# Two attention sink terms per pair of heads: from two ScalarE exponentials to one VectorE subtraction and one ScalarE exponential

## The chip, the cores and the metric

The kernel runs on one core of a Trainium2 chip. The metric is device time in microseconds (us) of one execution. Engines are named as in the profile: PE is TensorE's matmuls and PEld its weight loads, DVE is VectorE, ACT is ScalarE, POOL is GpSimd, SP is SyncE, whose queue issues the DMAs.

## The reference

Two layers, each one mixer sub-layer over 1024 latent tokens and 256 context tokens of width 1024, in float32: a modulated RMS norm, one input projection to 2560 columns, three parallel branches (attention with 8 heads of 64, a depthwise convolution, a Fourier branch), each times a SiLU gate, one output projection, a gated residual. Only the attention's softmax matters here. Each block of 128 queries sees at most 384 local keys and the 256 context keys, and one more logit per head that has no value row, the sink:

```
s_sink = broadcast(sink.reshape(1, 1, N_KV_HEADS, GQA_GROUP, 1, 1))
p = softmax(concatenate([s_loc, s_ctx, s_sink], axis=-1), axis=-1)
```

So the denominator of a row is the sum of the exponentials of its 640 (or fewer) scores plus `exp(sink - max)`, where the maximum goes over scores and sink. That last term, one number per query and head, is what the change computes in another way.

## The kernel before

Every large product is split into three single-pass products of rounded halves, so PE carries most of the work: the input projection (lines 198 to 200) in 128x512 matmuls over eight blocks of the width, the output projection by the same lines.

Attention is a list of steps, one for each block of 128 queries and pair of heads: 40 steps in the first layer, 32 in the second, 72 in all. A step makes scores (PE, lines 899 and 901) into one of two PSUM tiles of two banks each; takes the negated maximum (`maxima`, DVE); makes the exponentials (`exponentials`, ACT, line 925), whose sum comes with a read of the accumulator; makes the two sink terms (`sinks`, ACT, line 933); adds and inverts (`divide`, two DVE operations of 128x2) and multiplies the exponentials by the inverse on POOL (line 941). One step later PE transposes the result (line 955), ACT copies the rounded half (`ph`, line 960), DVE takes the rest (`pl`); one more step later PE multiplies by the values (line 969). A score tile is free for the next head when its exponential has been read.

The signs are turned: the score tiles hold negated scores, so the maximum is a minimum, `st[:, j]` holds minus the maximum of head `j`, and `nsink` holds minus the sink logits of all 16 heads of both layers in every partition. The small tile `st` (128x10) of a step holds minus the maxima in columns 0 and 1, the sink terms, later the denominators, in 2 and 3, the sums in 4 and 5, the inverses in 6 and 7.

Between two steps stands a piece of other work: half a projection, splits of weights, the output projection of a block whose attention is done. The function `step` writes the order of a program, but what runs is the order that a list scheduler makes of it: it places each instruction on its engine by readiness in its own model of the machine, with the program's order as priority. Each engine then runs its list strictly in order. A moved instruction can therefore move others far from it, on every engine.

All VectorE operations go through a helper and carry line 57 in the profile, so they are told apart by the names of what they write: `st<-` with no source is the read of a maximum, `st<-st` of 128x2 the addition or the reciprocal of `divide`.

Of the kernel before, what the change touches and what calls it, by code (L numbers as in the profile page):

```python
# [15 lines left out]
AF = mybir.ActivationFunctionType  # L16
ALU = mybir.AluOpType
# [13 lines left out]
NH = 8  # L31
# [108 lines left out]
def tile_backbone(ctx: ExitStack, tc: tile.TileContext, a, out):  # L140
    nc = tc.nc
    V, S, G, T = Behind(tc, nc.vector), nc.scalar, nc.gpsimd, nc.tensor
# [30 lines left out]
    def fill_v(us):  # L173
        p0 = tc.cur_priority
        tc.cur_priority = p0 + 300
        V.background = True
        while back and us > 0:
            t, f = back.popleft()
            f()
            us -= t  # L180
        V.background = False
        tc.cur_priority = p0
# [4 lines left out]
    def flush(q):  # L187
        for _ in range(len(q)):
            q.popleft()()
# [294 lines left out]
    class Pair:  # L484
# [6 lines left out]
        def step(self, blocks=range(NK)):  # L491
            for k in blocks:
                ks = slice(k * P, (k + 1) * P)
                for oo, w in zip(self.o, self.w):
                    mm3(oo, (w[0][:, ks], w[1][:, ks]), (hx[k][0].cols(*self.c), hx[k][1].cols(*self.c)),
                        k == 0, k == NK - 1)
# [338 lines left out]
    nsink = const.tile([P, DEPTH * NH], F32, name="nsink")  # L835
# [9 lines left out]
    class Attention:  # L845
# [82 lines left out]
        def sinks(self, i):  # L928
            z, pr = self.st[i], self.steps[i][1]
            st = z["st"]  # L930
            for j in range(2):
                h = self.l * NH + pr * 2 + j
                S.activation(st[:, 2 + j:3 + j], nsink[:, h:h + 1], AF.Exp, scale=-1.0, bias=st[:, j:j + 1])

        def divide(self, i):
            z = self.st[i]
# [58 lines left out]
        def step(self, fill=None):  # L995

            i, n = self.next, len(self.steps)
            if i == n + 2:
                return False
            self.next += 1  # L1000
            c, d = 0 <= i - 1 < n, 0 <= i - 2 < n
            flush(post)
            if i < n:
                b, pr = self.steps[i]
                self.scores(i)
                self.maxima(i, 0)
                if pr == 3:
                    self.q.pop(b)[0].put()
                if pr == 0:
                    self.load(i + 4)  # L1010
            if c:
                self.transpose(i - 1, 0)
            if i < n:
                self.maxima(i, 1)
                self.exponentials(i, 0)
            if c:
                self.transpose(i - 1, 1)
            if d:
                self.values(i - 2)
            if i < n:  # L1020
                self.exponentials(i, 1)
            if c:
                self.transpose(i - 1, 2)
            if d:
                self.output(i - 2)
            if i < n:
                self.sinks(i)
                self.divide(i)
                if pr == 2:
                    self.queries(i + 2)  # L1030
            flush(late)
            fill_v(2.5)
            if fill:
                fill()
            return True
# [637 lines left out]
```

## Time and profile before

| | before |
|---|---|
| median of 3 runs | 1176.14 us (1173.57 to 1181.28) |
| profiled execution | 1175.1 us, its span 1172.9 us |
| busy share of the span | PE 93%, PEld 79%, DVE 71%, ACT 46%, POOL 24% |
| chain that ended last | PE 73%, DVE 12%, DMA 7%, ACT 3% |
| mean granted clock of PE | 0.97 of full |

The page's first part gives the busy time of each engine, its fourth part the chain of work that ended last, followed back from the last instruction; the share of an engine in that chain is the time in which that engine held up the end. A wait is told as the engine and line that waited, then who released it. Attention runs from about 275 to 625 us in the first layer and from about 845 to 1140 us in the second.

### The profile page before, as it was taken

How to read it: one execution, taken by the hardware profiler on the slowest of the kernel's cores; microseconds unless marked ns; L12 is line 12 of the kernel's file. 1: busy time of each engine (PE TensorE's matmuls, PEld its weight loads, DVE VectorE, ACT ScalarE, POOL GpSimd, SP SyncE). 2: the span in 40 equal slices, each digit the busy share in tenths (PEclk: the TensorE clock that was granted, in tenths of full speed). 3: DMA queues.
4: the chain of work that ended last, by engine and by line, in shares of the span. 5: the costliest groups of instructions: out<-in, count | busy, mean ns of one | idle time of the engine just before them, and what ended most of it. 6: DMA issues, size and time to landing. Idle time of an engine off the chain costs nothing.

```text
span 1172.9 us, 17178 instructions
## 1 busy us (share of the span) xinstructions
PE 1095.1 (93%) x6165; PEld 923.6 (79%) x6165; DVE 828.8 (71%) x1702; ACT 541.5 (46%) x1195; POOL 285.7 (24%) x271
## 2 busy tenths in 40 slices
PE   5999999999999999899999999989889997999986
PEld 2688887778878988788888788868678886788865
DVE  4545998997776567767665269999566677577763
ACT  4442222215566555555557653222346555455551
POOL 1230000002222234344553220000131344234321
PEclk9999999999999999899999999999989997899989
DMA  9711238453322253336458423532423254433210
GB/s 333 230 61 55 90 111 235 149 193 81 86 87 75 79 161 98 97 113 205 161 191 269 141 60 107 169 114 72 108 63 86 91 149 127 116 108 91 91 54 36
DMA packets 150924, 144.90 MB, mean 124 GB/s; under 512 B 7302, under 2 KB 128566, under 8 KB 150840
## 3 DMA queue, kind: packets, MB, share of 16 engines
q1 hardware_dynamic: 150840, 143.82, 40.5%
q8 instruction: 48, 0.79, 0.3%
q14 instruction: 36, 0.29, 0.1%
HBM read 109.71 MB, written 34.09 MB: 123 GB/s over the span
## 4 chain that ended last, share of the span: by engine, by line
PE 73%; DVE 12%; DMA 7%; ACT 3%; issue 2%; SPq 2%; POOL 1%; DVEq 0%; ACTq 0%; POOLq 0%
PE mm L198 13%; PE mm L199 13%; PE mm L200 13%; PE mm L969 5%; PE pt L955 5%; PE pt L198 5%; PE pt L199 5%; PE pt L200 4%; PE score L899 2%; PE score L901 2%; DMA wr<-od 2%; DVE score L57 2%; DVE cy L57 2%; DMA wada<-w_ada 1%; DVE pl L57 1%
## 5 line engine op out<-in xcount | busy, mean ns | idle before, releaser
L198 PE MATMUL mm<-hxh,wh 128*128 128x512 f32 (+1 forms) x808 | 312.4, 388 | 8.5 <-DVE t L57 4.5
L199 PE MATMUL mm<-hxl,wh 128*128 128x512 f32 (+1 forms) x808 | 309.4, 383 | 0.0
L200 PE MATMUL mm<-hxh,wl 128*128 128x512 f32 (+1 forms) x808 | 308.4, 382 | 0.0
L198 PEld LDWEIGHTS mm<-hxh,wh 128*128 128x128 f32 x808 | 154.2, 192 | 39.1 <-DVE t L57 5.9
L57 DVE SCALAR_TENSOR_TENSOR cy<-cu,cw,cy 128x1009 f32<-128x1009 f32 (+25 forms) x180 | 175.7, 1005 | 0.9
L200 PEld LDWEIGHTS mm<-hxh,wl 128*128 128x128 f32 x808 | 154.2, 191 | 27.6
L199 PEld LDWEIGHTS mm<-hxl,wh 128*128 128x128 f32 x808 | 154.5, 191 | 25.3 <-issue 0.5
L941 POOL TENSOR_SCALAR p<-p,st 128x640 f32<-128x640 f32 (+2 forms) x144 | 109.2, 771 | 261.9 <-DVE st L57 162.8
L57 DVE TENSOR_TENSOR pl<-pt,ph 128x512 fp32r<-128x512 f32 x184 | 111.9, 616 | 70.1 <-ACT ph L960 68.3
L409 POOL TENSOR_TENSOR wl<-wr,wh 128x512 fp32r<-128x512 f32 (+1 forms) x31 | 56.3, 1817 | 392.2 <-ACT wh L408 388.6
L960 ACT ACTIVATE ph<-pt 128x512 fp32r<-128x512 f32 x184 | 97.4, 541 | 112.4 <-PE pt L955 109.5
L925 ACT ACTIVATE p<-score,st 128x640 f32<-128x640 f32 (+2 forms) x144 | 105.5, 735 | 37.8 <-DVE st L57 36.6
L57 DVE CUSTOM_DVE_ANT_0 score<-score,mask,nsink 128x640 f32<-128x640 f32 (+2 forms) x144 | 111.1, 782 | 13.9 <-PE score L901 9.8
L408 ACT ACTIVATE wh<-wr 128x1024 fp32r<-128x1024 f32 (+1 forms) x74 | 61.8, 850 | 119.1 <-PE mm L199 72.0
L955 PE MATMUL pt<-ident,p 128*128 128x128 f32 x640 | 105.2, 283 | 11.2 <-DVE pl L57 7.8
L198 PE MATMUL pt<-hxh,wh 128*128 128x512 f32 (+1 forms) x296 | 110.7, 378 | 1.1 <-ACT gsum L341 1.1
L199 PE MATMUL pt<-hxl,wh 128*128 128x512 f32 (+1 forms) x296 | 109.4, 370 | 0.3 <-POOL hxl L400 0.3
L200 PE MATMUL pt<-hxh,wl 128*128 128x512 f32 (+1 forms) x296 | 108.3, 366 | 0.0
L969 PE MATMUL mm<-ph,v 128*128 128x256 f32 x320 | 91.5, 311 | 5.4 <-ACT ph L960 3.7
L955 PEld LDWEIGHTS pt<-ident,p 128*128 128x128 f32 x640 | 79.3, 145 | 21.9 <-issue 7.7
L969 PE MATMUL mm<-pl,v 128*128 128x256 f32 x320 | 92.9, 313 | 3.7 <-DVE pl L57 3.7
L969 PEld LDWEIGHTS mm<-ph,v 128*128 128x128 f32 x320 | 64.2, 201 | 8.9 <-ACT ph L960 5.9
(230 smaller groups left out, 1795.5 us busy)
## 6 DMA issues: line engine op xcount, KB each, us to landing
wada<-w_ada SPq DMA_DIRECT2D x48, 512.0 KB, 7.3
wr<-w_in SPq DMA_DIRECT2D x38, 512.0 KB, 4.1
qq<-qd SPq DMA_DIRECT2D x36, 256.0 KB, 4.5
x1d<-x SPq DMA_DIRECT2D x10, 512.0 KB, 3.8
xnd<-xr SPq DMA_DIRECT2D x10, 512.0 KB, 3.7
p<-xnd SPq DMA_DIRECT2D x10, 512.0 KB, 4.9
sg<-sgd SPq DMA_DIRECT2D x36, 128.0 KB, 3.0
wr<-yd SPq DMA_DIRECT2D x18, 256.0 KB, 4.3
```

Source lines behind the costliest of these rows:

```text
L57: r = f(*args, **kw)
L198: T.matmul(o, lhsT=lhs[0], rhs=rhs[0], start=start, stop=False)
L199: T.matmul(o, lhsT=lhs[0], rhs=rhs[1], start=False, stop=False)
L200: T.matmul(o, lhsT=lhs[1], rhs=rhs[0], start=False, stop=stop)
L408: S.activation(hi, raw, AF.Copy)
L409: (E or (G if holding[0] else V)).tensor_tensor(out=lo, in0=raw, in1=f32(hi), op=ALU.subtract)
L899: T.matmul(sc[:, c0:512], lhsT=q2[:, h, :], rhs=kx[:, k0:k0 + nl], start=fst, stop=not fst)
L925: S.activation(pp[:, j * n:(j + 1) * n], z["sc"][j][:, 768 - n:768], AF.Exp, scale=-1.0, bias=st[:, j:j + 1], accum_out=st[:, 4 + j:5 + j])
L941: G.tensor_scalar(out=pp[:, j * n:(j + 1) * n], in0=pp[:, j * n:(j + 1) * n], scalar1=st[:, 6 + j:7 + j], scalar2=1.0, op0=ALU.mult, op1=A ...
L955: T.transpose(out=bt[:, (j % 2 * 2 + y) * P:(j % 2 * 2 + y + 1) * P], in_=pp[:, c0:c0 + P], identity=ident)
L960: S.activation(ph, bt[:, :w], AF.Copy)
L969: T.matmul(o, lhsT=self.vv[kt][:, kv * P:(kv + 1) * P], rhs=y.cols(j * 256, (j + 1) * 256), start=(j == 0 and x == 0), stop=(j == z["nkt"] ...
```

## The change

`sinks` now makes both terms of a pair at once. One VectorE subtraction of 128x2 takes minus the sinks from minus the maxima into columns 2 and 3, and one ScalarE exponential of 128x2, in place and without scale and bias, makes the terms. Before, each head had its own ScalarE exponential of 128x1 that read the sink with scale -1 and the maximum as bias. In `step` the call moves from behind the second head's transposes and output to the place ahead of the second head's exponential.

```
         def sinks(self, i):
             z, pr = self.st[i], self.steps[i][1]
             st = z["st"]
-            for j in range(2):
-                h = self.l * NH + pr * 2 + j
-                S.activation(st[:, 2 + j:3 + j], nsink[:, h:h + 1], AF.Exp, scale=-1.0, bias=st[:, j:j + 1])
+            h = self.l * NH + pr * 2
+            V.tensor_tensor(out=st[:, 2:4], in0=st[:, 0:2], in1=nsink[:, h:h + 2], op=ALU.subtract)
+            S.activation(st[:, 2:4], st[:, 2:4], AF.Exp)
...
             if i < n:
+                self.sinks(i)
                 self.exponentials(i, 1)
             if c:
                 self.transpose(i - 1, 2)
             if d:
                 self.output(i - 2)
             if i < n:
-                self.sinks(i)
                 self.divide(i)
```

The scheduler makes these lists of it. First ScalarE in the first layer, at the step whose state is `st_3370` (`p5_3369` are its exponentials, `ph_196` and `ph_199` copies for the step before). Before:

```order
L636 ACTIVATE t512_3337<-cy_111_1362 128x256
L933 ACTIVATE st_3370<-nsink_87,st_3370 128x1 x2
L960 ACTIVATE ph_196_3288<-pt_3319 128x256
L925 ACTIVATE p5_3369,st_3370<-score_3371,st_3370 128x640
L925 ACTIVATE p5_3369,st_3370<-score_3376,st_3370 128x640
L505 ACTIVATE t512_3365<-mm_3340 128x512
L960 ACTIVATE ph_199_3382<-pt_3386 128x512
L960 ACTIVATE ph_199_3382<-pt_3395 128x512
```

Now:

```order
L636 ACTIVATE t512_3337<-cy_111_1362 128x256
L960 ACTIVATE ph_196_3288<-pt_3321 128x256
L925 ACTIVATE p5_3369,st_3370<-score_3371,st_3370 128x640
L505 ACTIVATE t512_3365<-mm_3340 128x512
L960 ACTIVATE ph_199_3382<-pt_3386 128x512
L925 ACTIVATE p5_3369,st_3370<-score_3376,st_3370 128x640
L960 ACTIVATE ph_199_3382<-pt_3395 128x512
L933 ACTIVATE st_3370<-st_3370 128x2
```

Both sink terms stood ahead of their step's exponentials and of a copy from PE's transposes; now their one successor stands behind the second exponential and behind a copy that waits for PE. Over all 72 steps, 42 of the 144 exponentials of sinks stood ahead of their step's first exponential before, and 10 of 72 stand ahead of it now; the other 62 stand behind the second one, none between the two. In 19 steps at least one ACT operation that waits for another engine's work stands between the second exponential and the sink; in 4 before.

VectorE at the same step. Before:

```order
L57 ISA score_3376,st_3370<-score_3376,mask_86,nsink_87 128x640
L57 ISA st_3370 128x1
L57 TENSOR_TENSOR ot_184_3015<-t512_3324,mm_3307 64x256
L57 SCALAR_TENSOR_TENSOR cy_84_979<-t512_3334,cy_84_979 128x256
L57 RECIPROCAL st_3275<-st_3275 128x2
L57 SCALAR_TENSOR_TENSOR cy_111_1362<-t512_3337,cy_111_1362 128x256
L57 TENSOR_TENSOR pl_198_3290<-pt_3319,ph_196_3288 128x256
L57 TENSOR_TENSOR st_3370<-st_3370 128x2
L57 RECIPROCAL st_3370<-st_3370 128x2
```

Now:

```order
L57 ISA score_3376,st_3370<-score_3376,mask_86,nsink_87 128x640
L57 ISA st_3370 128x1
L57 TENSOR_TENSOR pl_198_3290<-pt_3321,ph_196_3288 128x256
L57 SCALAR_TENSOR_TENSOR t512_3365<-t512_3365,mm_3340 128x512
L57 TENSOR_TENSOR st_3370<-st_3370,nsink_87 128x2
L57 TENSOR_TENSOR pl_201_3384<-pt_3386,ph_199_3382 128x512
L57 ISA score_3463,st_3462<-score_3463,mask_86,nsink_87 128x640
L57 ISA st_3462 128x1
L57 TENSOR_TENSOR pl_201_3384<-pt_3395,ph_199_3382 128x512
L57 TENSOR_TENSOR st_3370<-st_3370 128x2
L57 TENSOR_TENSOR ot_203_3413<-t512_3422,mm_3402 64x256
L57 RECIPROCAL st_3370<-st_3370 128x2
```

The subtraction stands two places behind the read of the second maximum, and the addition of the divide has moved behind the next step's first maximum. Over the 72 steps the addition stood on average 5.9 rows behind the second maximum before, and 7.5 rows behind it now; one of these 1.6 rows is the subtraction. The read of the second maximum and the subtraction stand next to each other in 18 steps, with one to three operations between in 47, and with four or five in 7.

PE's list holds the same 5243 rows in both, in another order from the first attention step on: mostly groups of four transposes (line 955) or of one head's scores that moved by some matmuls against the projections beside them.

## Rows read from the trace of the kernel before

**Rows 1.** The page: span, busy time by engine, chain that ended last.
```profile
span 1172.9 us, 17178 instructions
...
PE 1095.1 (93%) x6165; PEld 923.6 (79%) x6165; DVE 828.8 (71%) x1702; ACT 541.5 (46%) x1195; POOL 285.7 (24%) x271
...
PE 73%; DVE 12%; DMA 7%; ACT 3%; issue 2%; SPq 2%; POOL 1%; DVEq 0%; ACTq 0%; POOLq 0%
```

**Rows 2.** Busy time of PE, PEld, DVE, ACT, POOL by stage; then PE clock, DMA.
```profile
275.00:625.00 350.00, 334.72 (x1984) 295.50 (x1982) 243.91 (x591) 196.63 (x483) 129.13 (x129) 0.99 0.41 122
...
845.00:1140.00 295.00, 268.27 (x1474) 233.09 (x1475) 206.33 (x468) 162.30 (x380) 102.56 (x97) 0.93 0.34 98
```

**Rows 3.** Waits of PE: total us, times, longest.
```profile
PE score L899 <- ACT p L925: 14.7, 13, 3.3
...
PE pt L955 <- POOL p L941: 0.9, 1, 0.9
```

**Rows 4.** The same table for four stretches behind a long gap of PE.
```profile
848.00:859.00 11.00, 9.02 (x32) 7.55 (x33) 7.64 (x22) 6.74 (x20) 2.97 (x5) 0.53 0.07 25
967.00:975.00 8.00, 6.32 (x18) 5.23 (x19) 5.90 (x14) 3.00 (x8) 1.58 (x2) 0.57 0.62 197
991.00:1002.00 11.00, 8.04 (x33) 7.51 (x33) 10.88 (x19) 7.21 (x17) 6.08 (x4) 0.53 0.56 139
1131.00:1142.00 11.00, 9.66 (x39) 8.41 (x40) 6.00 (x14) 4.54 (x12) 3.99 (x5) 0.53 0.14 54
```

**Rows 5.** Timeline: PE's gaps (start, us, operation, idle before and releaser).
```profile
481.89 0.44 PE L899 MATMUL score<-kh,q 128*128 128x384 f32 x1 [2.46 <-ACT p L925]
...
849.33 0.58 PE L899 MATMUL score<-kh,q 128*128 128x256 f32 x1 [3.26 <-ACT p L925]
...
968.68 0.69 PE L899 MATMUL score<-kh,q 128*128 128x384 f32 x1 [2.98 <-ACT p L925]
...
993.03 0.45 PE L955 MATMUL pt<-ident,p 128*128 128x128 f32 x1 [3.78 <-DVE pl L57]
...
1132.06 0.58 PE L969 MATMUL mm<-pl,v 128*128 128x256 f32 x1 [2.07 <-DVE pl L57]
```

**Rows 6.** Timeline: ScalarE just ahead of the first three of these gaps' ends.
```profile
481.72 0.30 ACT L933 ACTIVATE st<-nsink,st 128x1 f32<-128x1 f32 x1
...
848.50 0.69 ACT L925 ACTIVATE p<-score,st 128x512 f32<-128x512 f32 x1 [1.70 <-DVE st L57]
...
967.74 0.79 ACT L925 ACTIVATE p<-score,st 128x640 f32<-128x640 f32 x1 [4.53 <-DVE st L57]
```

**Rows 7.** Groups by line: count, busy us, mean ns, idle before and releaser.
```profile
L933 ACT ACTIVATE st<-nsink,st 128x1 f32<-128x1 f32 x144 | 41.7, 290 | 25.0 <-DVE st L57 24.9
...
L57 DVE TENSOR_TENSOR st<-st 128x2 f32<-128x2 f32 x72 | 14.0, 195 | 20.3 <-ACT st L933 11.6 <-ACT p L925 8.4
```

**Rows 8.** Line 600, a small ScalarE copy without bias: ns min, median, max.
```profile
L600 ACT ACTIVATE ry<-pt x5: 155/161/173, 282.0 to 863.6; 128x4 f32<-128x4 f32 x4, 128x2 f32<-128x2 f32 x1
```

**Rows 9.** Timeline: the end of a step, ScalarE's second exponential, then VectorE's addition.
```profile
898.97 0.80 ACT L925 ACTIVATE p<-score,st 128x640 f32<-128x640 f32 x1
899.64 0.21 ACT L925 ACTIVATION_READ_ACCUMULATOR p<-score,st 128x1 f32 x1
...
899.89 0.16 DVE L57 TENSOR_TENSOR st<-st 128x2 f32<-128x2 f32 x1 [1.13 <-ACT p L925]
```

**Rows 10.** Timeline: the longest addition of a divide, and GpSimd beside it.
```profile
983.80 3.15 POOL L409 TENSOR_TENSOR hxl<-wor,hxh 128x512 fp32r<-128x512 f32 x2 [4.30 <-ACT hxh L408]
...
985.73 1.24 DVE L57 TENSOR_TENSOR st<-st 128x2 f32<-128x2 f32 x1
```

**Rows 11.** Waits of ScalarE and GpSimd: total us, times, longest.
```profile
ACT ph L960 <- PE pt L955: 109.5, 65, 3.6
...
ACT st L933 <- DVE st L57: 24.9, 26, 2.8
...
POOL p L941 <- DVE st L57: 162.8, 38, 13.4
```

More of the change, by code (lines that the diff above doesn't have):

```diff
@@ L930, in sinks @@
             st = z["st"]
-            for j in range(2):
-                h = self.l * NH + pr * 2 + j
-                S.activation(st[:, 2 + j:3 + j], nsink[:, h:h + 1], AF.Exp, scale=-1.0, bias=st[:, j:j + 1])
+            h = self.l * NH + pr * 2
+            V.tensor_tensor(out=st[:, 2:4], in0=st[:, 0:2], in1=nsink[:, h:h + 2], op=ALU.subtract)
+            S.activation(st[:, 2:4], st[:, 2:4], AF.Exp)
         def divide(self, i):
@@ L1020, in step @@
             if i < n:
+                self.sinks(i)
                 self.exponentials(i, 1)
@@ L1026, in step @@
             if i < n:
-                self.sinks(i)
                 self.divide(i)
```

## The prediction, made before the changed kernel ran

> **What bounds the kernel now.** The page comes first: PE is busy for 1095.1 of 1172.9 us, DVE for 828.8, ACT for 541.5, and the chain that ended last is PE's for 73%, DVE's for 12% and ACT's for 3% [rows 1]. The change touches DVE and ACT and adds no matmul, so it can win or lose only what PE does not do in its 93%, and what the clock takes from it.
>
> The table by stage comes next. In the first attention stage PE is busy for 334.72 of 350 us at a granted clock of 0.99, in the second for 268.27 of 295 at 0.93 [rows 2]. That leaves 15 and 27 us of idle PE, and in the second stage 7% of the clock. Then the waits of PE: the largest is for exponentials that free a score tile, 14.7 us in 13 times. For POOL's product, the end of the divide, PE waited once, for 0.9 us [rows 3].
>
> The last view is the timeline at the long gaps [rows 5]. The four in the second stage last 3.26, 2.98, 3.78 and 2.07 us, and in the 11, 8, 11 and 11 us behind them the granted clock is 0.53 to 0.57 on average, so PE runs most of that time on the lower of its levels, 1.2 GHz for 2.4 [rows 4]. What the clock takes there is (1 - 0.53) x 11 = 5.2 us, 3.4, 5.2 and 5.2. With 12.1 us of gaps that is 31.1 us for four places, **7.8 us each**. This number matters most below: a stall of 2 to 4 us costs twice its length, so a few of them outweigh all the small operations of this change.
>
> **The change part by part.** *Removed from ACT:* 144 exponentials of 128x1 at 290 ns, 41.7 us [rows 7].
>
> *Added to ACT:* 72 exponentials of 128x2 without a bias column, which the trace does not show. From above, the removed operation bounds it at 290 ns, the same function with such a column [rows 7]; from below, a 128x4 copy without one at 161 ns [rows 8]. I take 161, since size and operands are nearer to that row: 11.6 us, at most 20.9. ACT gets 30.1 us of work less, at least 20.8. The Trainium skill, ScalarE: Activation LUTs, section What ACT_TABLE_LOAD costs, states 186 ns plus 0.83 ns per element for an activation with constant scale and bias, and some 93 ns more for each column operand: by that estimate the new one takes 188 ns, 13.5 us in all, and the sum below rises by 0.1 us.
>
> *Added to DVE:* 72 subtractions of 128x2. The addition of the divide has the same shape and the same two kinds of operands and takes 195 ns on average, 14.0 us for 72 [rows 7]. They cost nothing if each falls into DVE's idle time, and the second slower rival below tells what they cost if none does.
>
> *What of it lies on the path:* DVE's 12% of the span is 141 us, 17% of its busy time; ACT's 3% is 35 us, 6.5% of its own [rows 1]. By these shares 14.0 us more of DVE are 2.4 us and 30.1 us less of ACT are 2.0 us (1.4 at the upper price). **The sum is +0.4 us.** PE's matmuls hide the rest; where PE waits for DVE or ACT there is no cover, and those places are in the shares.
>
> *The latency of a step:* the second exponential starts at 898.97, its accumulator is read until 899.85, and the addition starts at 899.89 [rows 9]; here the sinks had been made ahead of it. Now the one exponential comes behind in 62 steps, as the lists show. Where nothing stood behind before, the divide comes 0.2 us later; where a 290 ns sink stood behind, as in most steps, 0.13 us earlier. The subtraction needs no time of its own there, as long as it and the one operation that usually stands before it end within the roughly 0.9 us of exponential and read. These cancel within 0.1 us per step.
>
> *The moved call:* between the two exponentials, as the source says it, the sink ends up in no step. The first head's score tile is freed no later by it, and nothing is to be had or lost from that placement as such. No DMA is added. What does move is the list of every engine.
>
> *The moved lists* have no price of their own in the trace. They can make a long gap or remove one, at 7.8 us, and a single one either way would be no surprise.
>
> The profiled execution took 1175.1 us, 2.2 around its span of 1172.9; with +0.4 it is 1175.5. The median of the three runs is 1.0 above that execution and the runs lie between 1173.57 and 1181.28, so I forecast **1176 us, no change**, with a range of its own of one long gap either way, 1168 to 1184.
>
> **Rivals.** *Faster: ACT no longer blocks itself.* Before, a sink at the head of ACT's list waited for a maximum 26 times, 24.9 us in all [rows 11], with everything behind it held, and now only ten sinks stand ahead of their exponentials. If the three gaps for a score tile went (2.46, 3.26 and 2.98 us [rows 5]) with the lower clock behind two of them (5.2 and 3.4), 17 us would go, and two long gaps fewer by the new lists give 16: 1160. For it speaks that this is PE's largest wait. Against it speak the rows ahead of those gaps: at 848.50 and 967.74 ACT had been idle for 1.70 and 4.53 us until DVE delivered a maximum, and only at 481.72 does a 0.30 us sink stand in the way [rows 6]. DVE is late there, and DVE gets more to do. Chance 0.22.
>
> *Slower: the divide is held behind copies.* In 19 steps, against 4, the sink stands behind ACT operations that wait for other engines, mostly a copy from the transposes, and DVE's addition, now further down its in-order list, waits for it with the next step's maxima and remainders behind. A copy waits for the transposes 1.7 us on average (109.5 in 65 times [rows 11]), so 19 x 1.7 = 32 us of later divides. POOL already waits 162.8 us for divides [rows 11] and would only start later; PE's transposes one step on are the end that matters. Against it: PE waited for POOL once [rows 3], so there is slack of a part of a step. It decides from about seven of the 19 delays reaching PE, 12 us; at half of them the time is 1192. Chance 0.14.
>
> *Slower: GpSimd holds the subtraction.* At 985.73 an addition of 128x2 took 1.24 us and ended just after a 3.15 us stretch of two POOL operations [rows 10]. POOL is busy for 129.13 of 350 and 102.56 of 295 us, 36% [rows 2]; the additions mostly escape since POOL is waiting for them, but the subtraction comes earlier in the step, when POOL may be at a weight split. If 36% of the 72 are caught, 26, for half of a 1.6 us operation, DVE loses 21 us, with the next maximum queued behind. By DVE's share on the path that is 3.6 us and within the forecast; with two thirds on the path it is 14 us, 1190. It decides where more than half lands on PE. Chance 0.08. The Trainium skill, SBUF — State Buffer, section SBUF: two separate sides, states such a rule: a VectorE operation with two SBUF inputs and a GpSimd operation that reads SBUF exclude each other for the whole instruction. By that rule all 26 are caught; the trace agrees at 985.73.
>
> **How the numbers follow.** About 1% is what a measurement of this kernel tells from no change. The forecast has 0.56, the faster rival 0.22, the two slower ones 0.14 and 0.08. The range takes in the forecast's own and reaches to the middle of the rivals on both sides: 1159 to 1193, which leaves out roughly half of each, 2 in 10. Faster by over 1% has 0.22, within 1% has 0.56, slower by over 1% has 0.22.
>
> **What would show it.** Right: ACT's busy time about 30 us lower (20 to 30), DVE's about 14 higher, the subtraction near 195 ns, the exponential near 161; PE's idle time in the two stages near 15 and 27 us, with about as many long gaps and the clock at 0.99 and 0.93. The faster rival shows as fewer waits of PE for a score tile with a higher clock in the second stage; the first slower one as waits of PE's transposes for POOL, of more than a few us in all; the second as subtractions of over 0.5 us beside POOL's splits, with PE waiting for DVE behind them. The prediction is wrong if the new lists make or remove two or more long gaps: what those cost is measured above, where they fall is not.

## The result: 0.5% slower, where no change was forecast

| | before | changed |
|---|---|---|
| median | 1175.45 us (22 runs, 1168.63 to 1184.74) | 1182.77 us (22 runs, 1177.93 to 1187.22) |
| ratio, 95% interval | | 1.0053, 1.0037 to 1.0069 |
| span of the profiled execution | 1172.9 us | 1180.6 us |
| mean granted clock of PE | 0.97 | 0.97 |

The change costs 6 to 7 us. That lies within the 1% that the prediction called no change, but the interval leaves out 1: it is a loss.

### The profile page after: what moved, and what is told of

It is laid out like the page before. It is cut to its first block, busy times and chain, and to the rows that moved or that the text cites. A ratio compares the mean times of both kernels' runs of the same rounds, so it can differ in the third digit from the quotient of the medians.

```text
span 1180.6 us, 17185 instructions
## 1 busy us (share of the span) xinstructions
PE 1094.3 (93%) x6165; PEld 921.9 (78%) x6165; DVE 842.9 (71%) x1774; ACT 523.1 (44%) x1123; POOL 285.0 (24%) x271
## 4 chain that ended last, share of the span: by engine, by line
PE 72%; DVE 11%; DMA 8%; issue 3%; ACT 2%; SPq 2%; POOL 1%; DVEq 0%; ACTq 0%; POOLq 0%
PE mm L198 13%; PE mm L199 12%; PE mm L200 12%; PE pt L198 5%; PE pt L199 5%; PE pt L200 5%; PE mm L969 4%; PE pt L955 4%; PE score L899 2%; DVE score L57 2%; DMA wr<-od 2%; PE score L901 2%; DVE pl L57 1%; DMA od<-ot 1%; DMA wor<-w_out 1%
## 5 line engine op out<-in xcount | busy, mean ns | idle before, releaser
L955 PE MATMUL pt<-ident,p 128*128 128x128 f32 x640 | 104.0, 279 | 14.7 <-DVE pl L57 11.0
L955 PEld LDWEIGHTS pt<-ident,p 128*128 128x128 f32 x640 | 78.5, 144 | 25.6 <-issue 9.6
```

What stands on the lines that cost most here:

```text
L955: T.transpose(out=bt[:, (j % 2 * 2 + y) * P:(j % 2 * 2 + y + 1) * P], in_=pp[:, c0:c0 + P], identity=ident)
```

## The profile after

The page's first and fourth part, against [rows 1]:

```profile
span 1180.6 us, 17185 instructions
...
PE 1094.3 (93%) x6165; PEld 921.9 (78%) x6165; DVE 842.9 (71%) x1774; ACT 523.1 (44%) x1123; POOL 285.0 (24%) x271
...
PE 72%; DVE 11%; DMA 8%; issue 3%; ACT 2%; SPq 2%; POOL 1%; DVEq 0%; ACTq 0%; POOLq 0%
```

ACT lost 18.4 us of busy time and DVE gained 14.1, and PE's own work is the same: the 7.7 us of span are PE's idle time. The table by stage says where, against [rows 2]:

```profile
275.00:625.00 350.00, 329.76 (x1929) 291.17 (x1928) 246.97 (x613) 183.41 (x435) 126.96 (x126) 0.97 0.39 117
845.00:1140.00 295.00, 265.41 (x1467) 230.52 (x1466) 207.90 (x485) 150.69 (x340) 98.23 (x93) 0.94 0.35 102
```

In the first attention stage PE is idle for 20.2 us where it was for 15.3, and its clock is 0.97 for 0.99; in the second 29.6 for 26.7, at a clock that is no lower. The costs of the small operations, from the groups by line (count, busy us, mean ns, idle before), against [rows 7]:

```profile
L57 DVE TENSOR_TENSOR st<-st,nsink 128x2 f32<-128x2 f32 x72 | 22.8, 316 | 0.8
L933 ACT ACTIVATE st<-st 128x2 f32<-128x2 f32 x72 | 14.4, 200 | 27.8 <-DVE st L57 27.3
L57 DVE TENSOR_TENSOR st<-st 128x2 f32<-128x2 f32 x72 | 13.1, 182 | 11.2 <-ACT st L933 5.8 <-ACT p L925 4.8
```

The new exponential takes 200 ns. The subtraction takes 316 ns on average, though its median is 154: 17 of the 72 last for more than 250 ns, up to 1848. The waits of PE (total us, times, longest), against [rows 3]:

```profile
PE score L899 <- ACT p L925: 11.3, 9, 3.1
PE pt L955 <- DVE pl L57: 11.0, 6, 6.5
PE mm L198 <- DVE t L57: 9.8, 5, 3.6
...
PE mm L969 <- DVE t L57: 5.4, 1, 5.4
...
PE pt L955 <- POOL p L941: 3.3, 4, 2.2
```

The wait for ACT's exponentials is shorter than before (14.7 us). Waits for DVE have taken its place; two of them before:

```profile
PE pt L955 <- DVE pl L57: 7.8, 9, 3.8
PE mm L198 <- DVE t L57: 4.5, 3, 2.9
```

Among them stands one gap of 6.5 us, the longest of both attention stages. Nearly all of the loss is there when the second layer's attention begins: its first exponential starts 6.5 us later than the 848.50 of before [rows 6]:

```profile
855.03 0.69 ACT L925 ACTIVATE p<-score,st 128x512 f32<-128x512 f32 x1 [1.70 <-DVE st L57]
```

The gap itself, on the timeline (start, us, engine, line, operation, idle before and releaser):

```profile
439.36 0.63 ACT L408 ACTIVATE hxh<-wor 128x512 fp32r<-128x512 f32 x1 [3.55 <-DMA wor<-w_out]
...
441.20 0.43 DVE L57 CAST hxh<-wor 128x512 fp32r<-128x512 f32 x1 [2.14 <-DMA wor<-w_out]
441.67 0.69 DVE L57 TENSOR_TENSOR hxl<-wor,hxh 128x512 fp32r<-128x512 f32 x1
442.27 0.89 DVE L57 CUSTOM_DVE_ANT_0 score<-score,mask,nsink 128x640 f32<-128x640 f32 x1
...
443.08 0.69 DVE L57 TENSOR_TENSOR pl<-pt,ph 128x512 fp32r<-128x512 f32 x1
...
443.91 1.09 PE L955 MATMUL pt<-ident,p 128*128 128x128 f32 x4 [6.47 <-DVE pl L57]
```

PE waits for a `pl` that stands in DVE's list behind a cast of `w_out`, and that cast waits with an empty DVE for a DMA. ACT waits in the same way, in the first of these lines. Before, in that place:

```profile
437.83 0.38 PE L969 MATMUL mm<-ph,v 128*128 128x256 f32 x1 [2.02 <-ACT ph L960]
...
439.26 0.43 DVE L57 CAST hxh<-wor 128x512 fp32r<-128x512 f32 x1 [1.03 <-DMA wor<-w_out]
...
442.29 0.41 PE L955 MATMUL pt<-ident,p 128*128 128x128 f32 x2 [0.72 <-DVE pl L57]
442.86 0.69 DVE L57 TENSOR_TENSOR pl<-pt,ph 128x512 fp32r<-128x512 f32 x1
...
443.69 0.63 PE L955 MATMUL pt<-ident,p 128*128 128x128 f32 x4 [0.99 <-DVE pl L57]
```

The same cast stood ahead of the same maximum and the same `pl` there too. What differs is PE's list: between the projection and the group of four transposes that waits at last, it had 29 matmuls before and has 15 now. So before, PE still had work while the cast waited, and lost 3.73 us in three waits instead of 6.47 in one.

## Experiments

Two main theories at first: LISTS, the order in which the engines' work now stands, and OPS, the operations themselves. A third, ROUND TRIP, is the way from DVE to ACT and back ahead of the divide. To part them, a program's lists are written out and held: each instruction gets an edge from the one ahead of it on its engine, which orders the issue and waits for nothing.

```
+    for text in ORDER.values():
...
+            tc.add_manual_dep(i, last.name, mybir.DependencyInfo(
+                mybir.DependencyClass.NoSync, mybir.DependencyReason.DATA), reason="order")
```

Given its own lists, the program before comes out the same row for row. Each ratio is to runs of the kernel before beside it; that median lay between 1173.2 and 1178.0 us from one group of runs to the next, so two experiments of different groups can differ by 0.2 to 0.3% for that alone.

| run | operations | lists | ratio, 95% interval |
|---|---|---|---|
| changed | new | changed | 1.0053, 1.0037 to 1.0069 |
| e1 | new | before | 1.0051, 1.0023 to 1.0078 |
| e2 | old | changed | 1.0046, 1.0024 to 1.0069 |
| e3 | old | own, call moved | 0.9882, 0.9857 to 0.9906 |
| e4 | new | changed in layer 1, before in layer 2 | 1.0060, 1.0037 to 1.0082 |
| e5 | no subtraction | before | 0.9987, 0.9964 to 1.0010 |
| e6 | one-input subtractions | before | 1.0021, 0.9996 to 1.0046 |
| e7 | new | e3 | 0.9979, 0.9951 to 1.0007 |
| e8 | new | changed, three rows moved | 1.0017, 0.9994 to 1.0041 |
| e9 | old | e3 in layer 1, before in layer 2 | 0.9929, 0.9903 to 0.9955 |
| e10 | old | before in layer 1, e3 in layer 2 | 0.9957, 0.9935 to 0.9978 |
| e11 | old | e3, four short moves | 0.9892, 0.9865 to 0.9919 |
| e12 | no subtraction | changed | 1.0084, 1.0052 to 1.0116 |
| e13 | new, subtraction and exponential later | before | 1.0078, 1.0049 to 1.0106 |
| e14 | new, subtraction first | changed | 1.0105, 1.0076 to 1.0134 |
| e15 | new, subtraction and exponential later | e3 | 0.9935, 0.9910 to 0.9960 |

One thing needed no run: with the new operations and the call of `sinks` left at its old place, the scheduler makes the changed kernel's lists, row for row. The moved call does nothing in this change.

### Operations against lists: e1, e2, e4

e1, on the source before, with the lists of before:

```
-            for j in range(2):
-                h = self.l * NH + pr * 2 + j
-                S.activation(st[:, 2 + j:3 + j], nsink[:, h:h + 1], AF.Exp, scale=-1.0, bias=st[:, j:j + 1])
+            h = self.l * NH + pr * 2
+            V.tensor_tensor(out=st[:, 2:4], in0=st[:, 0:2], in1=nsink[:, h:h + 2], op=ALU.subtract)
+            S.activation(st[:, 2:4], st[:, 2:4], AF.Exp)
```

> The new subtraction and the new exponential, but every engine's list is that of the kernel before, written out: PE, POOL and SP row for row; on ACT the new exponential stands at the place of the later of the two old ones; on DVE the subtraction stands right behind the read of the second maximum. Theory LISTS (the 7 us come from the order in which the engines' work stands, not from the two operations): 1.000 of before, 0.998 to 1.002, and the 6.5 us gap of PE at 444 us shrinks to the 2 us of before. Theory OPS (72 subtractions of 0.15 to 0.2 us on DVE lie on the path, 14 us in all, about half of it shown): 1.005, 1.003 to 1.008. Theory ROUND TRIP (the addition of the divide comes later since subtraction and exponential pass between DVE and ACT): 1.002 to 1.005, with PE waiting for POOL's multiplications as long as in the changed kernel, 3.3 us, or more.

e2 is the reverse edit on the changed source, with the changed kernel's lists:

> The reverse: the two old exponentials of each pair, one behind the other at the place where the changed kernel has its one, no subtraction, and every other row of every engine's list as in the changed kernel. LISTS: 1.005 of before, 1.003 to 1.008 (the two old exponentials take 18 us more of ACT than the one, which may add a little), and the gap at 444 us stays at 5 us or more. OPS: 1.000, 0.998 to 1.002. ROUND TRIP: 1.000 to 1.002, since no subtraction has to come first; the addition stands as late on DVE's list as in the changed kernel.

Each half alone costs what both cost together: 1.0051 and 1.0046, against 1.0053. Neither LISTS nor OPS had that; each was right in half. ROUND TRIP wanted waits of PE for POOL of 3.3 us or more in e1 and no loss in e2; these waits are 1.3 us in e1, and e2 loses. In e2 the trace follows the changed kernel's within 2 us over the whole span, and the long gap is there:

```profile
442.96 1.09 PE L955 MATMUL pt<-ident,p 128*128 128x128 f32 x4 [6.06 <-DVE pl L57]
```

So the loss of the changed kernel is the loss of its lists. What the operations cost in the lists of before is another matter, and does not add to it (e12).

e4 joins two lists at a place where every engine has the same rows behind it in both:

> The new operations; each engine's list is the changed kernel's up to the first scores of the second layer's attention and that of e1_new_ops_old_lists from there on. LISTS, as the traces line up (the changed kernel loses 6.5 us up to there and 1 to 5 us, partly given back, behind it): 1.0055 of before, 1.003 to 1.007, the same as the changed kernel within 0.2%. OPS: 1.005, as all lists give. ROUND TRIP: between 1.002 and 1.005.

1.0060 agrees, but with e1 at 1.0051 it says little: both halves of the joined list cost 0.5%.

### What the subtraction costs: e5, e6, e12

```
-            V.tensor_tensor(out=st[:, 2:4], in0=st[:, 0:2], in1=nsink[:, h:h + 2], op=ALU.subtract)
-            S.activation(st[:, 2:4], st[:, 2:4], AF.Exp)
+            S.activation(st[:, 2:4], st[:, 0:2], AF.Exp)
```

> The lists of the kernel before with the new exponential of 128x2, and no subtraction at all: the exponential reads minus the maxima themselves, so the sinks are left out of the denominators. It takes away the 72 subtractions of e1_new_ops_old_lists (25.6 us of DVE, 29 of them over 250 ns, each ending 15 to 23 ns behind an instruction of POOL) and nothing else. If the subtraction is what made that kernel slower: 1.000 of before, 0.997 to 1.002; less than 0.997 would say that the 20 to 30 us that ACT saves are worth something by themselves. If not the subtraction but the new place or form of the exponential made it slower: 1.005 again.

0.9987 against 1.0051: in the lists of before the subtraction is the whole cost, 0.64%, some 7.5 us. And the ACT time saved is worth nothing that can be measured.

Why 72 operations of 160 ns may weigh so much shows in their durations. In e1, subtraction and GpSimd at one place of the second layer:

```profile
953.17 2.39 POOL L409 TENSOR_TENSOR wl<-wr,wh 128x1024 fp32r<-128x1024 f32 x1 [3.46 <-ACT wh L408]
953.57 0.14 DVE L57 DVE_READ_ACCUMULATOR2_ANT st<- 128x1 f32 x1
953.74 1.84 DVE L57 TENSOR_TENSOR st<-st,nsink 128x2 f32<-128x2 f32 x1
955.50 0.68 DVE L57 SCALAR_TENSOR_TENSOR t<-t,mm 128x512 f32<-128x512 f32 x1
```

POOL's split began at 953.17 and ended at 955.56; the subtraction, begun at 953.74, ended at 955.58. The `t` behind it, which frees a bank for the next projection matmul, came 1.7 us late, and that matmul waited 0.86 us for it, where before it did not wait. In e1 29 subtractions began inside a POOL instruction that had 0.2 us or more to run; all 29 ended 6 to 23 ns behind its end. The 72 took 25.6 us in all. e6 puts two operations with one tensor input each in that place:

```
+            for j in range(2):
+                V.tensor_scalar(out=st[:, 2 + j:3 + j], in0=st[:, j:j + 1], scalar1=nsink[:, h + j:h + j + 1], scalar2=None, op0=ALU.subtract)
```

> The lists of the kernel before with the new exponential, the subtraction as two VectorE operations of 128x1 that each read one tensor and take the sink of the head as a scalar of each partition. If POOL holds only operations that read two tensors (before, 6 of 72 additions of 128x2 took over 250 ns, and none of the 72 reciprocals, which read one): none of the 144 over 250 ns, and 144 x 0.12 to 0.16 = 17 to 23 us on DVE. HELD (the waiting behind POOL, 13.9 us over 29 subtractions, is what costs): 1.000 to 1.002. SUM (what counts is DVE's busy time, held or not): 1.003 to 1.006.

The same place in e6:

```profile
950.47 2.41 POOL L409 TENSOR_TENSOR wl<-wr,wh 128x1024 fp32r<-128x1024 f32 x1 [3.41 <-ACT wh L408]
950.87 0.14 DVE L57 DVE_READ_ACCUMULATOR2_ANT st<- 128x1 f32 x1
950.87 0.39 DVE L57 TENSOR_SCALAR st<-st,nsink 128x1 f32<-128x1 f32 x2
951.17 0.68 DVE L57 SCALAR_TENSOR_TENSOR t<-t,mm 128x512 f32<-128x512 f32 x1
...
952.37 0.53 DVE L57 TENSOR_TENSOR st<-st 128x2 f32<-128x2 f32 x1
```

Beside the same split the two run through in 0.39 us, while the addition of the divide, with two inputs, is held to 952.90, just behind the split's end. Over the kernel (ns min/median/max, first and last start), e1 and then e6:

```profile
L57 DVE TENSOR_TENSOR st<-st,nsink x72: 160/163/1837, 275.1 to 1141.4; 128x2 f32<-128x2 f32 x72
```
```profile
L57 DVE TENSOR_SCALAR st<-st,nsink x144: 197/213/216, 277.1 to 1137.6; 128x1 f32<-128x1 f32 x144
```

None of the 144 lasts for more than 250 ns, as expected. That is the rule of the Trainium skill (SBUF — State Buffer, section SBUF: two separate sides) that the prediction weighed: two SBUF inputs on VectorE against a GpSimd operation that reads SBUF. The rule has exceptions in the changed kernel, where 18 of the 20 subtractions that began so were held and two ran on beside a multiplication of line 941. One of them:

```profile
290.04 0.87 POOL L941 TENSOR_SCALAR p<-p,st 128x512 f32<-128x512 f32 x1
290.27 0.15 DVE L57 TENSOR_TENSOR st<-st,nsink 128x2 f32<-128x2 f32 x1
```

The time of e6, 1.0021, stands between the two theories and apart from neither: unheld, but at 213 ns each the 144 add up to 30.4 us, more than the 25.6 of the 72 and more than the 17 to 23 expected. Whether the holding or the sum of DVE's time counts stays open.

> The changed kernel's own lists with the 72 subtractions taken away (the exponential reads minus the maxima, so the sinks are left out of the denominators) and nothing else moved; the counterpart of e5_no_subtraction. If the subtraction costs the changed kernel's lists what it cost the lists of the kernel before (0.64%: 1.0051 with it, 0.9987 without): 0.997 to 1.001. If the lists, which were made with the subtraction in them, hide it and their own order costs the 0.5%, as e2_old_ops_new_lists (1.0046) says: 1.003 to 1.005, with the 6.5 us gap at 444 us as it was.

1.0084, above both expectations, though its interval meets that of the changed kernel. Taking the subtraction away gains nothing in these lists. The profiled execution is the slowest of its six; of its 8.2 us more span, 8.0 had arisen by 257 us, behind waits for the first stage's weights, where no list differs, and from there to 1083 us it follows the changed kernel within 2.2 us. So the 0.5% of the changed kernel is its lists' and not its subtractions'.

### The one long gap: e8

```
 DVE  hxl<-wor,hxh
-DVE  hxh<-wor (last cast of the burst)
-DVE  hxl<-wor,hxh
 DVE  score,st<-score,mask,nsink
 DVE  pl<-pt,ph
 DVE  ot<-t,mm
 DVE  score,st<-score,mask,nsink
+DVE  hxh<-wor (last cast of the burst)
+DVE  hxl<-wor,hxh
-ACT  hxh<-wor (last cast of the burst)
 ACT  ph<-pt
 ACT  t<-mm (two rows)
 ACT  ph<-pt
+ACT  hxh<-wor (last cast of the burst)
```

> The changed kernel with three rows of its lists moved, in the burst of w_out splits before the 6.5 us gap at 444 us: on DVE the last cast and subtraction of the burst (which wait 2.1 us for a DMA) go behind the next step's two maxima and the pl between them, on ACT the last cast (which waits 3.6 us for a DMA) goes behind the four operations for PE that stood behind it. LISTS with this gap as the main loss: the gap goes to 2.5 us or less and the time from 1.0053 to 1.001, 0.999 to 1.003. If the loss is not in this gap, or is given back behind it: 1.004 to 1.006.

The gap fell to 3.21 us (2.5 or less was expected), and the trace's lead over the changed kernel's grew from 1.2 us at 348 us to 7.9 us at 544:

```profile
437.66 0.68 DVE L57 TENSOR_TENSOR pl<-pt,ph 128x512 fp32r<-128x512 f32 x1
...
438.49 0.63 PE L955 MATMUL pt<-ident,p 128*128 128x128 f32 x4 [3.21 <-DVE pl L57]
...
439.40 0.41 DVE L57 CAST hxh<-wor 128x512 fp32r<-128x512 f32 x1
```

13 us around the gap in the table by window, changed kernel and then e8 (PE, PEld, DVE, ACT, POOL busy; clock, DMA):

```profile
437.00:450.00 13.00, 6.53 (x29) 5.94 (x28) 9.01 (x19) 4.72 (x11) 5.23 (x6) 0.74 0.69 193
```
```profile
434.00:447.00 13.00, 9.39 (x57) 8.04 (x56) 9.79 (x22) 5.64 (x13) 5.66 (x6) 1.00 0.63 197
```

The idle DVE is used, and the lower clock behind the gap is gone with it: 0.74 to 1.00. Three rows give back 0.36 of the 0.53%, some 4 us: 1.0017 against 1.0053. The two intervals just overlap, and the profiled execution is the fastest of e8's twelve, so its lead is larger than the gain; what it shows is the place. The rest of the lists' loss is not located. A second long gap that the kernel before does not have stands in the second layer of the changed kernel, and in e2 and e8 it is as long (5.40 us):

```profile
1010.48 0.55 PE L969 MATMUL mm<-ph,v 128*128 128x256 f32 x1 [5.39 <-DVE t L57]
```

DVE was busy all through the 10 us before it. What it costs was not tested.

### The place of the subtraction: e7, e13, e14, e15

Other lists, made without a subtraction (the edit is that of e1, on the lists of e3):

> The new operations in the lists of e3_old_ops_moved_call (0.988 of before): PE, POOL and SP row for row, the exponential at the place of the later of its two, the subtraction right behind the read of the second maximum. If the two operations cost 0.5% in any list that was not made for them: 0.993, 0.991 to 0.996. If the order of the lists decides, and the operations hide where PE has slack: 0.988, 0.985 to 0.991.

0.9979 against 0.9882, above both expectations: there the operations cost 1.0%, in the changed kernel's lists nothing that shows. In e1 and e7 the subtraction stands right behind the second maximum in every step, in the changed kernel 1.5 rows further down on average. Three runs moved it. e14 moved it alone; e13 and e15 also put the exponential right behind the second head's, while in e7 it stood ahead of that one. Here e14, at the step shown with the change:

```
 DVE  score,st<-score,mask,nsink
+DVE  st<-st,nsink
 DVE  pl<-pt,ph
 DVE  t<-t,mm
-DVE  st<-st,nsink
```

> The changed kernel (1.0053) with one thing moved: in the 54 of 72 steps where rows stand between the read of the second maximum and the subtraction (1.9 rows on average), the subtraction goes right behind the read. PLACE: it now costs here what it costs in e1_new_ops_old_lists: 1.010 to 1.013. PRICE, or these lists have the slack for it: 1.004 to 1.007.

> e1_new_ops_old_lists (1.0051) with two things moved in 71 of the 72 steps: the subtraction stands up to three rows behind the read of the second maximum on DVE (124 rows in all, 1.7 on average) instead of right behind it, and the new exponential stands right behind the second head's on ACT. All other rows as before. PLACE (a subtraction right behind the maximum stands ahead of the row of pl or t that PE waits for, and further down it costs nothing): 0.999 to 1.002. PRICE (72 more DVE rows cost 0.6% wherever they stand): 1.003 to 1.007.

> e7_new_ops_e3_lists (0.9979) moved as in e13_old_lists_sub_later: the subtraction up to three rows later (127 rows over 71 steps), the exponential right behind the second head's. PLACE: 0.988 to 0.991, the time of these lists with the old operations (0.9882). PRICE: 0.996 to 1.000.

e14 came out as PLACE says: 1.0105, 0.5% above the changed kernel, and its waits of PE for `t` grew from 9.8 to 12.6 us:

```profile
PE mm L198 <- DVE t L57: 12.6, 8, 3.8
PE pt L955 <- DVE pl L57: 12.0, 8, 6.7
```

e15 regained about half of e7's cost by the ratios, more by the medians (1165.80 for 1174.80 us, with 1163.03 in e3). Whether that is the subtraction's place or the exponential's, no run parts. e13 regained nothing and lies above both expectations: 1182.89 for 1182.41 in e1; PE's waits for `t` and `pl` fell there too, by 2.5 us, but those for other rows of DVE rose by 3.7. So the place of the subtraction counts in the changed kernel's lists, may count in e3's, and is not all. What the new operations cost goes with the list that they stand in: nothing that shows in the changed kernel, 0.5% more in e14, 0.6 in the lists of before, 1.0 in e3's.

### The moved call alone: e3, e9, e10, e11

e3 is the diff's other part, with the two old exponentials:

```
             if i < n:
+                self.sinks(i)
                 self.exponentials(i, 1)
...
-                self.sinks(i)
                 self.divide(i)
```

> The call of sinks moved ahead of the second head's exponential as in the change, with the two old exponentials; the scheduler makes lists of its own, which differ from both kernels' in far more rows than theirs from each other. LISTS: a third order, so a third time, anywhere within 1% of before on either side; it says how far a reshuffle alone moves the time. OPS and ROUND TRIP: 1.000, 0.998 to 1.002, as no operation is new.

0.9882: 14 us faster than before, from the order alone, beyond the 1% expected. With e11 it is the fastest of all, and beats both kernels. Its page:

```profile
span 1165.4 us, 17188 instructions
...
PE 1090.1 (94%) x6165; PEld 919.2 (79%) x6165; DVE 827.4 (71%) x1702; ACT 542.3 (47%) x1195; POOL 291.6 (25%) x271
```

Its engines do the work of before. PE is busy for 5.0 us less with the same matmuls; its mean granted clock is 0.976 for 0.972, which is 0.4% and of that size.

> Two old exponentials as before. Each engine's list is that of e3_old_ops_moved_call (0.988 of before) up to the first scores of the second layer's attention, and that of the kernel before from there on. By the traces of the two, the order of the first layer gives 6 of the 7.5 us between them (1.6 of these are there before any row has moved) and the second layer the rest: 0.993, 0.990 to 0.996. If the second layer's order makes it: 0.998 to 1.002.

> The reverse: the lists of the kernel before in the first layer, those of e3_old_ops_moved_call in the second. If the orders' prices simply add, the ratios of this and of e9_e3_lists_layer0 multiply to 0.988: 0.995 here, 0.992 to 0.998. If the first layer makes all of it: 1.000, 0.998 to 1.002.

0.9929 x 0.9957 = 0.9887: the gains of the two layers add, as expected. Which rows make them was not found.

> e3_old_ops_moved_call with four short moves on DVE's list and nothing else: at its gaps of PE at 465, 986 and 1037 us a pl and an ot that stood behind splits of w_out or behind the chain of the norm's inverse root go ahead of them, at 961 us a maximum goes ahead of a cast of w_out. If gaps made by the lists are what moves this kernel's time: the four gaps (12.1 us together) fall to 1 us or less each, with the half-clock stretches behind them: 8 to 14 us less, 0.976 to 0.982 of before. If what is won at one gap is waited for at the next: 0.985 to 0.989.

0.9892, no gain over e3: the second expectation. The four gaps did fall, from 12.1 to 2.6 us, but new ones stand right behind two of them (PE, e11):

```profile
468.76 0.66 PE L955 MATMUL pt<-ident,p 128*128 128x128 f32 x4 [2.73 <-DVE pl L57]
471.05 0.69 PE L899 MATMUL score<-kh,q 128*128 128x384 f32 x1 [1.52 <-ACT p L925]
```
```profile
983.82 0.58 PE L969 MATMUL mm<-ph,v 128*128 128x256 f32 x1 [4.33 <-ACT ph L960]
```

A reason why this failed and e8 worked can be read from e3's table by window at these two places:

```profile
459.00:473.00 14.00, 11.72 (x74) 10.97 (x72) 13.87 (x24) 7.54 (x16) 7.11 (x5) 0.88 0.47 131
980.00:993.00 13.00, 7.27 (x33) 6.66 (x32) 12.88 (x22) 7.50 (x16) 8.12 (x5) 0.65 0.44 125
```

DVE is busy for 13.87 of 14 us and 12.88 of 13, so a row that goes ahead there pushes another back that may be waited for as well. At the changed kernel's gap DVE was busy for 9.01 of 13 us and waited for a DMA, so the rows moved into idle time. That is argued from one gap that was mended and two that were not; it was not tested by itself, and two of the three new gaps wait for ACT and not for DVE.

## Why the prediction was wrong

- **The moved lists, put at nothing in the sum.** This step failed. That they "have no price of their own in the trace" is true, but the sum took them at 0, and they are the whole of the result: with the old operations in the changed kernel's lists e2 comes to 1.0046, 5.4 us, and without the subtraction (e12) those lists are no faster. The text named the lists as what would make it wrong, and allowed for one long gap either way. PE's gaps of over 2 us in the two attention stages are eight for seven before, but two of them, 6.47 and 5.39 us, are longer than any before (3.78). By e8's runs, taking 3.3 us off the first is worth 4 us. The price of 7.8 us for a gap is on the high side: it charges the lower clock for the whole of the 41 us behind the four gaps, while PE was busy for 33.0 of them [rows 4].
- **What bounds.** Right: PE's busy time is the same, and the loss is PE's idle time, with DVE behind it.
- **ACT's relief.** The exponential takes 200 ns, in its bounds of 161 to 290, but not near the 161 taken; 188, the estimate by the Trainium skill's page (ScalarE: Activation LUTs, section What ACT_TABLE_LOAD costs), is closer. By the groups ACT has 41.7 - 14.4 = 27.3 us less; its busy time fell by 18.4, less than the 20 to 30 said, since neighbours overlap in the records. It is worth nothing that can be measured (e5).
- **The 72 subtractions at 195 ns, 14.0 us.** Mis-sized: 22.8 us, and 25.6 and 25.9 in e1 and e7. That DVE's busy time rose by just the 14.1 forecast is luck: other rows took 3.4 us less in the new order, and more of the rows overlap in the records. The addition was the wrong model: it mostly escapes POOL, as the prediction said itself, and the subtraction does not.
- **Shares of the path, +0.4 us.** In the changed kernel's lists the operations cost nothing that shows, as the sum had it. In other lists the step fails: by DVE's share even 25.6 us would be 4.4, but the operations cost 7.5 us in the lists of before and 11.4 in e3's. A share of busy time on the chain does not say which of DVE's rows PE waits behind.
- **The moved call.** Nothing to be had or lost, right for this change, where the lists are the same with the call unmoved. With the old operations it is worth 14 us.
- **The rivals.** *Faster*: PE's wait for score tiles fell from 14.7 to 11.3 us, but DVE took the time. *Divide held behind copies*: PE's wait for POOL rose from 0.9 to 3.3 us, far from the 16 us of that rival. *GpSimd holds the subtraction*: the mechanism came with less than its size (26 subtractions and 21 us foreseen; here 17 of over 250 ns, 11.7 us above the median, in e1 29 and 13.9 us) and had a chance of 0.08. It is not what made the changed kernel slower (e12). In e1 the subtraction is the whole loss, but how much of that is the holding stays open (e6), and in e7 it was not tested.

## What to carry to other kernels

Under a list scheduler an edit of a few small operations is first of all a new order. Part the two by holding the lists, and give the order a price of its own: here it was worth 0.988 to 1.005 with the same operations, and the operations nothing to 1.0%. Before moving rows to mend a long gap, look whether the engine behind it is idle at the time: where it was, the move paid, and where it was full, the wait moved on. And a tiny two-input VectorE operation can cost what GpSimd is doing beside it.

## What the runs showed of the hardware

- A VectorE operation of 128x2 with two tensor inputs that began inside a GpSimd instruction with 0.2 us or more to run lasted to that instruction's end in 29 of 29 cases of e1, up to 1.84 us for 0.16, and in 18 of 20 of the changed kernel; the other two began beside a multiplication of line 941 and took 153 and 147 ns. With one tensor input and a scalar per partition (e6), all 60 that began so were done before that instruction's end, in 216 ns at most.
- The form with the scalar is dearer by itself: 213 ns in the median for 128x1, against 163 for 128x2 with two tensors that is not held (e1).
